# A hand-ordered encoder layer: another order for the first four rows of the sequence and for the last partial sums

## The chip, the core and the metric

One NeuronCore of one Trainium2 chip runs the whole layer in one launch. The metric is the device time of one execution in microseconds (us). The engines are named as in the profile: PE is TensorE (matmul), PEld its weight loads, DVE is VectorE, ACT is ScalarE, POOL is GpSimd, SP is SyncE, whose queue issues most DMAs.

## The reference

```python
memn = rms_norm(mem, mem_norm_g); h = x                       # x: (1, 512, 1024), mem: (1, 256, 1024)
n = rms_norm(h, mix_norm_g); proj = n @ w_in                  # 1024 -> 4608 columns
xa, zu, zv = proj[..., :512], proj[..., 512:1536], proj[..., 1536:2560]
gate_a, gate_b = sigmoid(proj[..., 2560:3584]), sigmoid(proj[..., 3584:])
ya = s5_branch(xa, ...)        # two scans over the sequence, GLU
yb = sgu_branch(zu, zv, ...)   # gelu, layer norm, 128x128 position mixing by head
h = h + (gate_a * (ya @ w_proj_a) + gate_b * (yb @ w_proj_b)) @ w_out
h = h + memory_cross_attention(rms_norm(h, xattn_norm_g), memn, w_q, w_k, w_v, w_xo)
n = rms_norm(h, ffn_norm_g); h = h + (silu(n @ w_gate) * (n @ w_up)) @ w_down
return rms_norm(h, final_norm_g)
```

All arrays are float32.

## The kernel before

**Products.** The 512 positions are four row tiles of 128 (t = 0 to 3). Each float32 operand is split into a high part in fp32r (a cast on ACT, `whi`, `xn_hi`) and the remainder (a subtraction on DVE, `wlo`, `xn_lo`); `mm3` makes a product of three passes: high by high, high by low of the second operand, low by high. `split` issues the cast and the subtraction. Weights come from HBM by SP's queue into `raw` tiles of 512 KB, three of them in rotation; `plan` lists every weight block in the order of use, and `next_w` loads ahead of the use and splits two blocks ahead (`SPLITS`). There are three `whi` and three `wlo` buffers, so a cast waits until PE has used the block three before.

**Order.** A scheduler that models the engines' times sets the order of the instructions on each engine. `in_order` (`tc.keep_in_program_order`) pins an instruction to the program's order, and `tc.issue_after(x)` puts the instructions of a block behind x on x's engine.

**The start (L617 to L692).** `g_mix` is the gain of the first norm, spread to 128 partitions by two matmuls into `pg`. `first_rows` norms and turns rows 0 and 1, pinned: the sums of squares of a row (`row_sums`, two ACT instructions), the factor r (`rms_factor`: two small DVE instructions and a power on POOL), the scaling by r and gain (`scaled`, on DVE, by halves of 512 columns), four transposes on PE into `ptr` (`to_feat`), and the split of `ptr` into `xn` (cast on ACT, subtraction on DVE). Among these stand the splits of the first three weight blocks w0, w1, w2 of `w_in` (`parts`, `split_w`), w0 by halves. Rows 2 and 3 follow in a loop, not pinned. The first product is `tokm` on `w_in` (four row tiles by 512 columns, two k blocks of 128 in each weight block). For row 0, the passes over w0 and w1 have an order of their own; an entry is (k block, part of `xn`, part of w):

```python
first=(((0, 0, 0), (0, 0, 1), (1, 0, 0), (0, 1, 0), (1, 1, 0), (1, 0, 1)),
       ((0, 0, 0), (1, 0, 0), (0, 1, 0), (1, 1, 0), (0, 0, 1), (1, 0, 1)))
```

`behind=turned1` puts row 0's passes over the later blocks behind the last transpose of row 1.

**The end (L1926 to L1984).** The down projection of the FFN is made of seven products (`DOWN`), each over six chunks of `w_down`. Products 7 and 4 are the last ones. `row_by_row` takes two chunks for row tile t = 0 and then for t = 1. After product 7, `onto_h` takes its two PSUM tiles `dx` off `h`, and `first_half(t, 0)` for t = 2, 3 makes the sum of squares of one half row (ACT), the half row times the last gain (DVE, `rest<-h,g_o`) and a small factor. Then product 4 goes over its chunks; its first two are again `row_by_row`.

Of the kernel before, what the change touches and what calls it, by code (L numbers as in the profile page):

```python
# [12 lines left out]
ALU = mybir.AluOpType  # L13
# [4 lines left out]
P = 128  # L18
D = 1024
T = 512  # L20
NT = T // P
# [31 lines left out]
def hybrid_layer_kernel(  # L53
# [38 lines left out]

    pinned, turned, row_tr = [False], [], [None]
    in_order = tc.keep_in_program_order
# [10 lines left out]
    def halves(src, place=None):  # L105
        _, k, n = src.shape
        if place is None:
            hi = wp.tile([P, k, n], F32R, tag="hi", name="whi", bufs=3)
            lo = wp.tile([P, k, n], F32R, tag="lo", name="wlo", bufs=3)
        else:  # L110
            hi, lo = sums_place(place, k, n)
        split(hi, lo, src)
        return hi, lo


# [17 lines left out]
    def plan_block(w, kb, k, c0, n, more=None, place=None, parts=1):  # L133
        got = {}

        def load():
            got["raw"] = wp.tile([P, k, n], F32, tag="raw", name="wraw", bufs=3)
            for i in range(0, k, k // parts):
                nc.sync.dma_start(got["raw"][:, i:i + k // parts], block(w, kb + i, k // parts, c0, n))

        def make():
# [247 lines left out]
    def load_raw(j):  # L389
        begin(j, j)  # L390
# [49 lines left out]
    def tokm(w, c0, act, nk, evac, ntok=NT, last=2, kpt=2, hook=None, cut=None, t0=0, behind=None, fine=False, first=()):  # L440
# [22 lines left out]
        for t in toks:  # L463
# [5 lines left out]
            else:  # L469
                with nullcontext() if behind is None or t > t0 else tc.issue_after(behind):  # L470
                    tok_block(ps[t], t, held, act, kpt, full, nw == last, True)
# [148 lines left out]
    nc.scalar.dma_start(xt[:, 0, HALF[1]], x[0:P, HALF[1]])  # L620
    for t in range(1, NT):
        load_raw(t - 1)
        nc.sync.dma_start(xt[:, t, :], x[t * P:(t + 1) * P])
    xn_hi, xn_lo = token_slot("xn")
    xn = (xn_hi, xn_lo)

    def first_rows():
# [9 lines left out]
        def gain_copy(q):  # L637
            in_order(nc.scalar.copy(g_mix[:, HALF[q]], pg[q]))

# [14 lines left out]
        scaled(0, 0, r, pg[0])  # L654
        gain_copy(0)
        high, low = parts(0)
        high(0)
        low(0)
        turn(0, 0)
        idles(3)  # L660
        high(1)
        low(1)
        scaled(0, 1, r, pg[1])
        r = rms_factor(row_sums(xt[:, 1, :]))
        high, low = parts(1)
# [8 lines left out]
        split_w(2)  # L674
        ss = row_sums(xt[:, 2, :])
        turn(1, 1)
        pinned[0] = False
        return ss

    ss = first_rows()  # L680
    turned1 = row_tr[0]
    ss3 = row_sums(xt[:, 3, :])
    for t in range(2, NT):
        r = rms_factor(ss)
        with tc.issue_after(turned[1].ins):
            for i in range(2):
                nc.vector.scalar_tensor_tensor(xt[:, t, HALF[i]], xt[:, t, HALF[i]], r, g_mix[:, HALF[i]], ALU.mult, ALU.mult)
        to_feat(xt[:, t, :], xn_hi, xn_lo, slice(t * P, (t + 1) * P))
        ss = ss3
    last_row = [x.ins for x in turned]  # L690
# [1234 lines left out]

    def onto_h(ps, t0, half, op):  # L1926
        for t in range(2):
            hs = h[:, t0 + t, HALF[half]]
            added = nc.vector.tensor_tensor(hs, hs, ps[t], op)
            first = added.ins if t == 0 else first  # L1930
        return first

# [26 lines left out]
    row_by_row(7, CHUNKS - 2)  # L1959
    held_back[0] = onto_h(dx, 2, 0, ALU.subtract)  # L1960
    for t in range(2, 4):
        first_half(t, 0)

    held = []
    row_by_row(4, 0)
    held_back[0] = None
    for c in range(2, CHUNKS):
        ops_ = next_w(w_down, 4, c)
        if c < CHUNKS - 2:
            rows_product(dx, 4, c, ops_, (0, 1), slice(0, 512), False, c == CHUNKS - 3)  # L1970
        else:
            held.append((c, ops_))
# [46 lines left out]
```

## Time and profile before

| | |
|---|---|
| median of 3 runs | 864.3 us (863.7 to 865.82) |
| profiled execution | 864.56 us |
| its span | 862.8 us |
| PE busy | 853.0 us, 5898 matmuls |
| DVE, ACT, POOL busy | 646.8, 475.1, 105.6 us |
| granted TensorE clock | 0.998 |

The profile is of one execution. Times in it are from the start of its span; 864.56 - 862.8 = 1.8 us of the execution's time lie around the span. A row of the timeline has the start, the duration, the engine, the line, the operation with out<-in, and in brackets the engine's idle time before it with what ended that; "x3" is three instructions merged into one row, whose duration is then that of the three together. A matmul's end is modelled; matmuls of 512 columns that wait for nothing start 0.23 us apart, transposes 0.11 us apart.

### The profile page before, as it was taken

Reading aid. Unit: us, or ns where it says so; the run is one execution under the profiler, and the core shown is the slowest. Engines: PE = TensorE matmul, PEld = TensorE weight load, DVE = VectorE, ACT = ScalarE, POOL = GpSimd, SP = SyncE. Lnnn points to the kernel's source line nnn. Section 1 sums busy time; section 2 is a strip of 40 time slices with the busy share of each in tenths; the row PEclk is TensorE's granted clock in tenths of the full one; section 3 lists DMA queues with packets and bytes.
Section 4 is the critical chain, followed back from the end, with each engine's and each line's share of the span. In section 5 each row is a group of like instructions: output and inputs, shape, how many; then the busy total and the mean of one; then the engine's idle time right before and its main releaser. Section 6 shows DMA issues by size and latency. Waiting matters only on the chain.

```text
span 862.8 us, 14842 instructions
## 1 busy us (share of the span) xinstructions
PE 853.0 (99%) x5898; PEld 760.4 (88%) x5898; DVE 646.8 (75%) x889; ACT 475.1 (55%) x704; POOL 105.6 (12%) x157
## 2 busy tenths in 40 slices
PE   8999999999999999999999999999999999999996
PEld 6788888888889988899899888999999999988885
DVE  5799589958848768679658556877876778899875
ACT  6544874276436644467557444655545454656573
POOL 1001155100611000110010000010111111000000
PEclk9999999999999999999999999999999999999999
DMA  7549379645638687945788153557699789686641
GB/s 242 176 110 259 77 191 273 155 124 192 158 91 228 170 221 227 259 124 151 219 250 227 59 168 77 147 150 181 162 230 236 190 221 240 181 232 204 199 153 49
DMA packets 110135, 155.40 MB, mean 180 GB/s; under 512 B 8985, under 2 KB 77105, under 8 KB 110002
## 3 DMA queue, kind: packets, MB, share of 16 engines
q1 hardware_dynamic: 91762, 128.27, 47.0%
q0 software_dynamic: 18016, 25.66, 18.8%
q8 instruction: 46, 0.75, 0.4%
q10 hardware_dynamic: 288, 0.52, 0.2%
q14 instruction: 23, 0.19, 0.1%
HBM read 148.70 MB, written 37.20 MB: 215 GB/s over the span
## 4 chain that ended last, share of the span: by engine, by line
PE 97%; DVE 1%; ACT 1%; issue 0%; DMA 0%; POOL 0%; POOLq 0%
PE pf L400 27%; PE pt L400 18%; PE px L1292 13%; PE pq L1292 6%; PE dx L400 6%; PE dq L400 3%; PE pv L1292 3%; PE gx L1292 3%; PE qx L1292 3%; PE dv L400 2%; PE py L1081 1%; PE psc L400 1%; PE po L400 1%; PE qq L1292 1%; PE gq L1292 1%; PE ptr L573 1%
## 5 line engine op out<-in xcount | busy, mean ns | idle before, releaser
L85 ACT CAST whi<-wraw 128x1024 fp32r<-128x1024 f32 x132 | 135.7, 1029 | 141.7 <-PE pf L400 37.7
L86 DVE TENSOR_TENSOR wlo<-wraw,whi 128x1024 fp32r<-128x1024 f32 x132 | 157.5, 1193 | 70.9 <-ACT whi L85 69.6
L400 PE MATMUL pf<-xn,whi 128*128 128x512 f32 x320 | 100.2, 393 | 0.0
L1292 PE MATMUL px<-fn,whi 128*128 128x256 f32 x480 | 83.3, 276 | 0.0
L1292 PEld LDWEIGHTS px<-fn,whi 128*128 128x128 f32 x480 | 72.5, 188 | 0.2
L86 DVE TENSOR_TENSOR wlo<-b,whi 128x1024 fp32r<-128x1024 f32 x40 | 48.9, 1223 | 29.4 <-ACT whi L85 29.4
L400 PEld LDWEIGHTS pf<-xn,whi 128*128 128x128 f32 x320 | 59.5, 188 | 12.6 <-issue 0.7
L85 ACT CAST whi<-b 128x1024 fp32r<-128x1024 f32 x40 | 42.1, 1053 | 51.7 <-PE px L1292 26.3
L1292 PE MATMUL px<-fn,wlo 128*128 128x256 f32 x240 | 66.4, 277 | 0.0
L400 PE MATMUL pf<-xn,wlo 128*128 128x512 f32 x160 | 62.7, 392 | 0.0
L1292 PE MATMUL pq<-s,whi 128*128 128x256 f32 x320 | 55.0, 276 | 0.0
L400 PE MATMUL dx<-whi,s 128*128 128x512 f32 x170 | 53.0, 390 | 0.0
L86 DVE TENSOR_TENSOR wlo<-t,whi 128x1024 fp32r<-128x1024 f32 x30 | 36.7, 1225 | 19.3 <-ACT whi L85 19.3
L85 ACT CAST whi<-t 128x1024 fp32r<-128x1024 f32 x30 | 31.6, 1054 | 35.2 <-PE pv L1292 12.6
L1292 PEld LDWEIGHTS pq<-s,whi 128*128 128x128 f32 x320 | 48.1, 188 | 0.0
L1292 PEld LDWEIGHTS px<-fn,wlo 128*128 128x128 f32 x240 | 45.1, 188 | 0.0
L1292 PE MATMUL pq<-s,wlo 128*128 128x256 f32 x160 | 44.2, 276 | 0.0
L400 PE MATMUL pt<-whi,xn 128*128 128x512 f32 x120 | 39.6, 401 | 0.3 <-ACT xn L85 0.2
L400 PEld LDWEIGHTS dx<-whi,s 128*128 128x128 f32 x170 | 31.8, 188 | 6.8 <-DVE s L86 0.3
L313 POOL DMA_DIRECT2D dsum<-in_w_down_dram x12 | 13.3, 1109 | 190.4 <-DMA dsum<-in_w_down_dram 190.4
L400 PEld LDWEIGHTS pf<-xn,wlo 128*128 128x128 f32 x160 | 30.0, 188 | 6.2
L400 PE MATMUL dx<-wlo,s 128*128 128x512 f32 x85 | 33.1, 391 | 0.9 <-DVE wlo L86 0.9
(484 smaller groups left out, 2331.7 us busy)
## 6 DMA issues: line engine op xcount, KB each, us to landing
wraw<-in_w_in_dram SPq DMA_DIRECT2D x34, 512.0 KB, 4.5
dsum<-in_w_down_dram SPq DMA_DIRECT2D x20, 512.0 KB, 6.5
wraw<-dsum SPq DMA_DIRECT2D x20, 512.0 KB, 3.7
b<-in_w_gate_dram SPq DMA_DIRECT2D x15, 512.0 KB, 5.4
b<-in_w_up_dram SPq DMA_DIRECT2D x15, 512.0 KB, 4.9
wraw<-in_w_down_dram SPq DMA_DIRECT2D x15, 512.0 KB, 4.8
dsum<-in_w_down_dram POOLq DMA_DIRECT2D x10, 512.0 KB, 7.6
dsum<-dsum POOLq DMA_DIRECT2D x10, 512.0 KB, 6.4
```

Source lines behind the costliest of these rows:

```text
L85: hi = nc.scalar.copy(dst_hi, src)
L86: lo = nc.vector.tensor_tensor(dst_lo, src, dst_hi.bitcast(F32), ALU.subtract)
L313: plan[j + step][1].append((0, lambda d=dst, x=more: nc.gpsimd.dma_start(d, x, accum_op=ALU.add)))
L400: last_mm[0] = nc.tensor.matmul(ps, a[x], b[y], start=start and i == 0, stop=stop and i == 2, skip_group_check=free)
L573: tr = nc.tensor.transpose(ps[:, j, :], src[:, k * P:(k + 1) * P], ident)
L1081: in_order(nc.tensor.matmul(ps[64 * j:64 * j + 64, :], a, b, start=g % 4 == k == 0, stop=k == 2, tile_position=(0, 64 * j), skip_group_che ...
L1292: nc.tensor.matmul(ps[:, j, :], a[x], b[y], start=start and j == k == i == 0, stop=k == 3 and i == 2, skip_group_check=True)
```

## The change

- **Queue of SP:** row 1 of x is loaded between the two halves of w0 (`row_load`), where it came behind both.
- **First rows:** the first half of `g_mix` is copied by DVE, behind `low(0)`, where ACT copied it ahead of `high(0)`. The scaling of row 0's second half and the sums and the factor of row 1 stand ahead of `high(1)` and `low(1)`, the split of the second half of w0.
- **Rows 2 and 3:** row 2's factor is made ahead of `turn(1, 1)`; row 3's sums are put behind the cast of `turn(1, 1)` on ACT; each half row is turned by a call of its own. `turned1` is a list now: in `tokm`, the last passes of row tile 0 stand behind the last transpose of row 1, those of row tile 1 behind the first half of row 2, those of row tile 2 behind the first half of row 3.
- **The end:** `split_log` keeps the instructions of each weight split. The second subtraction of `onto_h` after product 7 is put behind the `wlo` of the newest block split by then, and `first_half` of rows 2 and 3 is moved behind `row_by_row(4, 0)` and behind the second subtraction of `onto_h` and the split of a weight block. The tokens of later chunks wait for that second subtraction, where it was the first.

```diff
@@ halves
-        split(hi, lo, src)
+        split_log.append([x.ins for x in split(hi, lo, src)])
@@ plan_block, load
             for i in range(0, k, k // parts):
                 nc.sync.dma_start(got["raw"][:, i:i + k // parts], block(w, kb + i, k // parts, c0, n))
+                if parts > 1 and i == 0:
+                    row_load[0]()
@@ tokm
-                with nullcontext() if behind is None or t > t0 else tc.issue_after(behind):
+                with nullcontext() if behind is None or t - t0 >= len(behind) else tc.issue_after(behind[t - t0]):
@@ loads of x
-    for t in range(1, NT):
+    load_row = lambda t: nc.sync.dma_start(xt[:, t, :], x[t * P:(t + 1) * P])
+    row_load[0] = lambda: load_row(1)
+    load_raw(0)
+    for t in range(2, NT):
         load_raw(t - 1)
-        nc.sync.dma_start(xt[:, t, :], x[t * P:(t + 1) * P])
+        load_row(t)
@@ first_rows
         def gain_copy(q):
-            in_order(nc.scalar.copy(g_mix[:, HALF[q]], pg[q]))
+            in_order(nc.vector.tensor_copy(g_mix[:, HALF[q]], pg[q]) if q == 0 else
+                     nc.scalar.copy(g_mix[:, HALF[q]], pg[q]))
...
         scaled(0, 0, r, pg[0])
-        gain_copy(0)
         high, low = parts(0)
         high(0)
         low(0)
+        gain_copy(0)
         turn(0, 0)
         idles(3)
+        scaled(0, 1, r, pg[1])
+        r = rms_factor(row_sums(xt[:, 1, :]))
         high(1)
         low(1)
-        scaled(0, 1, r, pg[1])
-        r = rms_factor(row_sums(xt[:, 1, :]))
         high, low = parts(1)
...
         ss = row_sums(xt[:, 2, :])
+        r = rms_factor(ss)
         turn(1, 1)
+        turned1 = [row_tr[0]]
         pinned[0] = False
-        return ss
-    ss = first_rows()
-    turned1 = row_tr[0]
-    ss3 = row_sums(xt[:, 3, :])
-    for t in range(2, NT):
-        r = rms_factor(ss)
-        with tc.issue_after(turned[1].ins):
-            for i in range(2):
-                nc.vector.scalar_tensor_tensor(xt[:, t, HALF[i]], xt[:, t, HALF[i]], r, g_mix[:, HALF[i]], ALU.mult, ALU.mult)
-        to_feat(xt[:, t, :], xn_hi, xn_lo, slice(t * P, (t + 1) * P))
-        ss = ss3
+        with tc.issue_after(turned[0].ins):
+            ss = row_sums(xt[:, 3, :])
+        for t in range(2, NT):
+            with tc.issue_after(turned[1].ins) if t > 2 else nullcontext():
+                for i in range(2):
+                    sc = nc.vector.scalar_tensor_tensor(
+                        xt[:, t, HALF[i]], xt[:, t, HALF[i]], r, g_mix[:, HALF[i]], ALU.mult, ALU.mult)
+            r = rms_factor(ss) if t == 2 else None
+            turn(t, 0)
+            turned1.append(row_tr[0])
+            turn(t, 1)
+        return turned1
+    turned1 = first_rows()
@@ onto_h
-    def onto_h(ps, t0, half, op):
+    def onto_h(ps, t0, half, op, behind=None):
         for t in range(2):
             hs = h[:, t0 + t, HALF[half]]
-            added = nc.vector.tensor_tensor(hs, hs, ps[t], op)
-            first = added.ins if t == 0 else first
-        return first
+            with nullcontext() if behind is None or t == 0 else tc.issue_after(behind):
+                added = nc.vector.tensor_tensor(hs, hs, ps[t], op)
+        return added.ins
@@ after product 7
-    held_back[0] = onto_h(dx, 2, 0, ALU.subtract)
-    for t in range(2, 4):
-        first_half(t, 0)
+    held_back[0] = onto_h(dx, 2, 0, ALU.subtract, split_log[-1][1])
     held = []
     row_by_row(4, 0)
+    behind_all = [held_back[0]] + split_log[used_w[0] - 1 - len(tiles)]
     held_back[0] = None
+    with ExitStack() as waits:
+        for x in behind_all:
+            waits.enter_context(tc.issue_after(x))
+        for t in range(2, 4):
+            first_half(t, 0)
```

The orders of instructions move as follows. Lines are those of each kernel, so L533 before is L537 in the changed kernel, L648 is L656, L400 is L404, L479 is L483.

ACT at the start, before, from the sums of row 0: `sq,ss<-xt` are sums of squares, `whi<-wraw 128x512` the casts of w0's halves, `whi<-wraw 128x1024` those of w1 and w2, `xn<-ptr` the casts of turned half rows.

```order
L533 ACTIVATE sq,ss<-xt 128x512 x2
L638 COPY g_mix<-pg 128x512
L648 CAST whi<-wraw 128x512
L85 CAST xn<-ptr 128x4x128
L648 CAST whi<-wraw 128x512
L533 ACTIVATE sq,ss<-xt 128x512 x2
L648 CAST whi<-wraw 128x1024
L638 COPY g_mix<-pg 128x512
```

The same place in the changed kernel:

```order
L537 ACTIVATE sq,ss<-xt 128x512 x2
L656 CAST whi<-wraw 128x512
L85 CAST xn<-ptr 128x4x128
L537 ACTIVATE sq,ss<-xt 128x512 x2
L656 CAST whi<-wraw 128x512
L656 CAST whi<-wraw 128x1024
L646 COPY g_mix<-pg 128x512
```

The first copy of the gain is gone from ACT, and the two sums of row 1 have changed places with the cast of w0's second half.

PE from the second half of row 1 on, before: `ptr` are transposes, `pt0_262`, `pt1_263` and `pt2_264` the sums of row tiles 0, 1 and 2; `whi_194` and `wlo_195` are w2, `whi_146` is w0.

```order
L573 MATMUL ptr_203<-ident_87,xt_115 128x128 x4
L400 MATMUL pt0_262<-whi_194,xn_128 128x512
L400 MATMUL pt0_262<-wlo_195,xn_128 128x512
L400 MATMUL pt0_262<-whi_194,xn_128 128x512 x2
L400 MATMUL pt0_262<-wlo_195,xn_128 128x512
L400 MATMUL pt0_262<-whi_194,xn_128 128x512
L400 MATMUL pt1_263<-whi_194,xn_128 128x512
L400 MATMUL pt1_263<-wlo_195,xn_128 128x512
L400 MATMUL pt1_263<-whi_194,xn_128 128x512 x2
L400 MATMUL pt1_263<-wlo_195,xn_128 128x512
L400 MATMUL pt1_263<-whi_194,xn_128 128x512
L573 MATMUL ptr_222<-ident_87,xt_115 128x128 x4
```

In the changed kernel, where w0 is `whi_145`:

```order
L577 MATMUL ptr_208<-ident_87,xt_115 128x128 x4
L404 MATMUL pt0_262<-whi_194,xn_128 128x512
L404 MATMUL pt0_262<-wlo_195,xn_128 128x512
L404 MATMUL pt0_262<-whi_194,xn_128 128x512 x2
L404 MATMUL pt0_262<-wlo_195,xn_128 128x512
L404 MATMUL pt0_262<-whi_194,xn_128 128x512
L577 MATMUL ptr_227<-ident_87,xt_115 128x128 x4
L404 MATMUL pt1_263<-whi_194,xn_128 128x512
L404 MATMUL pt1_263<-wlo_195,xn_128 128x512
L577 MATMUL ptr_234<-ident_87,xt_115 128x128 x4
L404 MATMUL pt1_263<-whi_194,xn_128 128x512 x2
L404 MATMUL pt1_263<-wlo_195,xn_128 128x512
```

The eight transposes of row 2 have come apart into four ahead of row tile 1's passes over w2 and four behind the second of them; those of row 3 are parted in the same way around row tile 2's passes over w2.

DVE near the end, before: `wlo_8681` and `wlo_8687` are the low parts of the first two chunks of product 4, `h<-h,dx` the two subtractions of `onto_h`, `s2` the low part of the tokens for chunks 2 and 3, `rest<-h,g_o` belongs to `first_half`.

```order
L86 TENSOR_TENSOR wlo_8681<-wraw_8596,whi_8680 128x1024
L1929 TENSOR_TENSOR h_3419<-h_3419,dx0_7869 128x512
L86 TENSOR_TENSOR s2_8720<-a_low_5453,s2_8720 128x1024
L1889 TENSOR_TENSOR rest_7506<-h_3419,g_o_8009 128x512
L1890 TENSOR_SCALAR msq_8011<-hss_3434 128x1
L1929 TENSOR_TENSOR h_3419<-h_3419,dx1_7870 128x512
L86 TENSOR_TENSOR wlo_8687<-wraw_8622,whi_8686 128x1024
```

In the changed kernel:

```order
L86 TENSOR_TENSOR wlo_8681<-wraw_8596,whi_8680 128x1024
L1942 TENSOR_TENSOR h_3419<-h_3419,dx0_7869 128x512
L86 TENSOR_TENSOR wlo_8687<-wraw_8622,whi_8686 128x1024
L1942 TENSOR_TENSOR h_3419<-h_3419,dx1_7870 128x512
L86 TENSOR_TENSOR s2_8712<-a_low_5453,s2_8712 128x1024
L1901 TENSOR_TENSOR rest_7506<-h_3419,g_o_8009 128x512
L1902 TENSOR_SCALAR msq_8011<-hss_3434 128x1
```

The low part of chunk 1 has moved ahead of four instructions. On ACT at the same place the cast `whi_8686` has moved ahead of the sum of squares of `first_half`.

Behind the first rows the scheduler's order differs on all engines up to about the middle of the gates' products; the work is the same there, in other places. From there to the end of product 7, and behind product 4's first chunks, the orders are equal but for buffer numbers.

More of the change, by code (lines that the diff above doesn't have):

```diff
@@ L90, in split @@
         return hi, lo
-    pinned, turned, row_tr = [False], [], [None]
+    pinned, turned, row_tr, row_load = [False], [], [None], [None]
     in_order = tc.keep_in_program_order
@@ L111, in halves @@
             hi, lo = sums_place(place, k, n)
-        split(hi, lo, src)
+        split_log.append([x.ins for x in split(hi, lo, src)])
         return hi, lo
+    split_log = []
     APART = (48, 112)
```

## The prediction

> **What bounds the kernel now.** I read the page first, then the stretches, then who waits, and only then the timeline at the two places that the change touches. The page's busy line and five stretches (the columns are length, then busy time of PE, PEld, DVE, ACT and POOL, granted clock, DMA share, GB/s):
>
> ```profile
> PE 853.0 (99%) x5898; PEld 760.4 (88%) x5898; DVE 646.8 (75%) x889; ACT 475.1 (55%) x704; POOL 105.6 (12%) x157
> ...
> 8.59:14.00 5.41, 4.62 (x20) 3.03 (x21) 4.48 (x9) 4.06 (x9) 0.56 (x1) 1.00 1.04 333
> ...
> 40.00:60.00 20.00, 20.00 (x94) 16.56 (x93) 19.82 (x38) 10.00 (x21) 1.34 (x1) 1.00 0.56 151
> 60.00:100.00 40.00, 40.00 (x368) 33.55 (x367) 35.72 (x53) 24.85 (x38) 2.32 (x2) 1.00 0.71 184
> 100.00:840.00 740.00, 740.00 (x5193) 669.05 (x5192) 553.71 (x707) 407.68 (x583) 97.41 (x139) 1.00 0.68 184
> 840.00:843.00 3.00, 2.13 (x10) 1.47 (x9) 3.00 (x6) 2.85 (x6) 0.00 (x0) 1.00 0.00 0
> ```
>
> PE has no idle time between 40 and 840 us, at full clock. So the change can win only where PE stands still: in the first rows and at 840 to 843 us. All that PE waits for, from the view of waits (total, times, longest), says the same:
>
> ```profile
> PE dx L400 <- DVE wlo L86: 0.9, 1, 0.9
> PE pt L479 <- ACT whi L648: 0.7, 1, 0.7
> ```
>
> **The change, part by part. 1: row 0 and the first weights.** The timeline of before; each row is one step of the chain:
>
> ```profile
> 6.95 0.59 ACT L638 COPY g_mix<-pg 128x512 f32<-128x512 f32 x1 [1.86 <-DVE xt L634]
> 7.17 0.60 PE L573 MATMUL ptr<-ident,xt 128*128 128x128 f32 x4
> 7.95 0.59 ACT L85 CAST xn<-ptr 128x512 fp32r<-128x512 f32 x1
> 8.59 0.50 PE L479 MATMUL pt<-whi,xn 128*128 128x512 f32 x1
> 8.95 0.64 ACT L533 ACTIVATE sq<-xt 128x512 f32<-128x512 f32 x1
> 10.03 0.50 PE L479 MATMUL pt<-wlo,xn 128*128 128x512 f32 x1
> 10.19 1.03 ACT L648 CAST whi<-wraw 128x1024 fp32r<-128x1024 f32 x1
> 11.27 1.19 PE L479 MATMUL pt<-whi,xn 128*128 128x512 f32 x4 [0.74 <-ACT whi L648]
> 12.37 1.09 PE L573 MATMUL ptr<-ident,xt 128*128 128x128 f32 x8
> 13.50 0.72 PE L479 MATMUL pt<-wlo,xn 128*128 128x512 f32 x2
> 14.54 0.62 PE L400 MATMUL pt<-whi,xn 128*128 128x512 f32 x2
> ```
>
> The gain copy leaves ACT, so the cast of `xn` waits for the transposes alone. Row 2's, below, has its cast 0.64 us after the first transpose (20.04 to 20.68); by that it starts at 7.17 + 0.64 = 7.81, and the first product at 8.59 - 0.14 = 8.45. On DVE the copy is new. No DVE copy of this shape from PSUM is in the trace; its bounds are ACT's 0.59 above and the 0.68 of a DVE subtraction from PSUM (shown at 840.48 below). It starts behind `low(0)`, which no longer waits for the gain copy, and either way ends by about 8.4, ahead of the 8.45 at which `xn_lo` can start; its price is nothing, or up to 0.2 if the first weight half lands late.
>
> Now the two sums of row 1 come ahead of the second cast of w0. Steps on ACT as now (cast to next 0.48, two sums 1.24 from 8.95 to 10.19): sums from 8.29, second half cast from 9.53 to 10.16. PE's third pass needs it and moves from 9.1 to 10.21: a new hole of 1.1 us. The next three passes follow at 0.34, 0.23 and 0.23, the last at 11.01. The cast of w1 runs from 10.05 to 11.08; PE asks for it at 11.24. So the hole of 0.74 closes and the sum of both is near zero: four passes to 11.93, transposes at 12.16 in place of 12.37. That is -0.21, because the scaling of row 1 (needed here) is done at about 11.55, a POOL power earlier than now. The next wait also goes: `wlo` of w1 now ends at 12.68, so passes go on at 13.15 in place of 13.50; and row 1's pass with `xn_lo` stands at 14.18 in place of 14.54: **-0.36**.
>
> All this needs row 1 of x by 8.29. The view of DMAs around 2.5 us has the time from issue to landing:
>
> ```profile
> xt<-in_x_dram SPq DMA_DIRECT2D x1, 512.0 KB, 6.0
> wraw<-in_w_in_dram SPq DMA_DIRECT2D x1, 256.0 KB, 4.6
> ```
>
> The first was issued at 2.49 and landed at 8.48, the second (w0's second half, ahead of it) at 2.02 and 6.66: 1.82 us for the 512 KB behind it. With 256 KB less ahead I estimate a landing at 8.48 - 0.7 to 0.9 = 7.6 to 7.8, and no wait. If it stayed at 8.48, the term would shrink by 0.2. [...] The landings above agree with the queue's order, so I keep the first.
>
> **2: rows 2 and 3.**
>
> ```profile
> 16.68 0.15 DVE L542 TENSOR_TENSOR ms<-ss 128x1 f32<-128x1 f32 x1
> 16.83 0.60 PE L573 MATMUL ptr<-ident,xt 128*128 128x128 f32 x4
> 17.17 0.55 POOL L544 TENSOR_TENSOR r<-ms,mhalf 128x1 f32<-128x1 f32 x1 [5.64 <-DVE ms L543]
> 17.18 0.48 PE L400 MATMUL pt<-whi,xn 128*128 128x512 f32 x1
> 18.08 0.69 DVE L86 TENSOR_TENSOR xn<-ptr,xn 128x512 fp32r<-128x512 f32 x1 [0.17 <-ACT xn L85]
> 18.69 1.41 DVE L687 SCALAR_TENSOR_TENSOR xt<-xt,r,g_mix 128x512 f32<-128x512 f32 x2
> 20.04 1.03 PE L573 MATMUL ptr<-ident,xt 128*128 128x128 f32 x8
> 20.68 1.08 ACT L85 CAST xn<-ptr 128x512 fp32r<-128x512 f32 x2 [2.62 <-PE ptr L573]
> 21.32 0.50 PE L400 MATMUL pt<-whi,xn 128*128 128x512 f32 x1 [0.24 <-ACT xn L85]
> 22.04 0.30 PEld L400 LDWEIGHTS pt<-whi,xn 128*128 128x128 f32 x2 [0.43 <-DVE xn L86]
> ```
>
> Now row 2 is turned late: PE goes from the transposes straight to passes that need them, and waits for cast and subtraction (its weight load, PEld, shows the second wait; 20.04 to 22.04 is 2.00 us for eight transposes and two passes; 8 x 0.11 + 2 x 0.23 = 1.34 would do). After: r of row 2 is done 0.24 earlier, at 17.48, as DVE's chain is; its scaling stands ahead of row 1's last `xn_lo` and runs 17.53 to 18.94. PE has six passes of row tile 0 from 16.81 to 18.27, waits at most 0.1 for the first half row, turns it (0.35, as 16.83 to 17.18), does two passes, turns the second half, and does the last four passes of row tile 1 (behind `xn_lo` of row 1, now late, at 19.5; PE comes there at 19.5). Meanwhile row 2 is cast and subtracted, by 20.5 for the first half. Row tile 2 starts at 20.55 and its third pass comes at 21.0 in place of 22.04: **-1.0** with the -0.36 in it. Row 3 is the same with no wait in it now; a group of four transposes and the switch back costs 0.35 + 0.09, so parting eight costs 0.2 more or less. I take **-0.95** for the start, from -0.2 (landing late, the new hole longer than the old) to -1.3.
>
> **3: the end.**
>
> ```profile
> 838.82 0.62 PE L400 MATMUL dx<-whi,s 128*128 128x512 f32 x2
> 838.79 0.63 ACT L533 ACTIVATE sq<-h 128x512 f32<-128x512 f32 x1 [0.94 <-DVE h L1929]
> 839.42 1.98 ACT L85 CAST whi<-wraw 128x1024 fp32r<-128x1024 f32 x2
> 840.48 0.68 DVE L1929 TENSOR_TENSOR h<-h,dx 128x512 f32<-128x512 f32 x1
> 841.07 1.22 DVE L86 TENSOR_TENSOR wlo<-wraw,whi 128x1024 fp32r<-128x1024 f32 x1
> 842.35 0.50 PE L400 MATMUL dx<-wlo,s 128*128 128x512 f32 x1 [0.87 <-DVE wlo L86]
> ```
>
> The cast of chunk 1 (839.42) waits for PE to leave its buffer: the first of the two passes at 838.82 is the last user and ends at 838.82 + 0.39 = 839.21. Without the sum of squares ahead it starts at 839.27 and ends at 840.3; the low part, no longer behind `rest` and the second subtraction, runs 840.35 to 841.57, and PE goes on at 841.62 in place of 842.35: **-0.73**. PE would ask at 841.3, so 0.3 stays. What is late next: the token low part moves from 838.7 to about 842.1 to 843.3; its first use is behind the last pass of 24 over chunks 0 and 1, after 845.8. The low part of chunk 2 ends at 845.2, used at 846.0. Both covers hold with 0.8 us or more. Bounds -0.5 to -0.9 (0.87 is the whole wait).
>
> **4: the middle**, up to about 285 us, is shuffled by the scheduler. PE has nothing to win there but small switches. The one queue with a new wait is POOL: its accumulating DMA of `qsum`, which waits for SP's transfer, now stands ahead of the layer norm's powers:
>
> ```profile
> 124.21 1.21 POOL L313 DMA_DIRECT2D qsum<-in_w_q_dram  x1 [2.50 <-DMA qsum<-in_w_q_dram]
> ...
> 125.70 2.18 ACT L1194 ACTIVATE zt<-zt,r 128x1024 f32<-128x1024 f32 x2
> ...
> L1256 PE MATMUL psv<-wsx,zt x17: 270/275/275, 148.1 to 149.9; 128*128 128x128 f32 x17
> ```
>
> The first power can then not start before about 125.4, ACT's scaling slips by up to 1 to 2 us, and the weight casts queued behind it; PE uses `zt` only at 148.1, and splits run two blocks ahead. I price it at 0, up to 1.
>
> **The sum:** -0.95 - 0.73 + 0 = -1.7 us against this execution's 864.56: 862.9. It lies 0.26 above the median, so the forecast against 864.3 is **862.6 us**. Bounds together (-0.2 - 0.5 + 1, and -1.3 - 0.9) give +0.3 to -2.2.
>
> **The rivals.**
> *The middle gives too.* If the new order also closes switches and short waits between 28 and 290 us, another 1.3 us: 861.3. For: each change from 512-column passes to small products costs about 0.1 to 0.2. Against: PE reads 100% there, and the changed order has three such groups more, not fewer.
> *DVE late, slower.* In 40 to 60 us DVE is busy 19.82 of 20.00, and in 60 to 100 35.72 of 40. The new order puts some four weight subtractions (1.22 each) ahead of products of the S5 branch, whose results PE's queue takes at fixed places with the dense passes behind. If PE gets there first, each costs up to 1.22, 4.9 in all: 862.6 + 4.9 = 867.5. It decides where that slip is more than the lead that the products have now; PE's zero idle there says that today's lead is enough, not how large it is.
> *The start does not do what it should.* The new hole at 9.1 to 10.2 grows by a late landing, and the gain of row 2 is lost on the late `xn_lo` of row 1: only the end remains, 864.3 - 0.73 = 863.6.
> *The clock falls.* PE now stands for 1.1 us after only two passes, right after the warm-up matmuls; if the grant halved, about six passes would take 0.23 longer each, 1.4: 864.0. The grant is 1.00 in 8.59 to 14.00 with a hole of the same length in it. [...]
>
> **How the numbers follow.** About 0.3%, 2.6 us, is what a measurement of this kernel can tell from no change: below 861.7 is faster, above 866.9 slower. Forecast 0.56 (its own range 861.2 to 863.7), of which 0.12 lies below 861.7, since the medians of three runs here scatter by some 0.7; the middle gives too 0.22, all faster; the start fails 0.08 and the clock 0.04, both the same; DVE late 0.10, slower. Faster 0.34, same 0.56, slower 0.10. The range of 860.9 to 864.8 leaves out DVE late and the tails.
>
> **What would show it.** Right: the first product at 8.45, the third pass near 10.2, no wait for ACT at w1, row tile 2's third pass near 21.0, PE's wait for `wlo` near 842 down to 0.3. Wrong: PE waits for S5 products between 40 and 290 us, or row 1's sums starting after 8.5.

## The result, and the profile after

Over 12 executions each the kernel after takes 869.14 us (866.02 to 871.62) and the kernel before 865.36 us (863.7 to 866.75), medians; the ratio is 1.0041, 95% interval 1.0028 to 1.0055. The change makes the kernel 0.4% **slower**; 0.2% faster was forecast. The profiled execution took 867.14 us with a span of 865.4, 2.58 us more than that of before.

One thing has to be known to read the times below: the executions of every kernel here, before's too, fall in two groups 2 to 3 us apart, by how fast PE's passes are at the start (the four that broadcast g take 2.14 us in before's profile and 3.78 in that of experiment 1; the last section shows the rows), so kernels are compared within a group. Groups are parted at the widest gap in a kernel's sorted times (in 8 at the second widest, since its profiled execution, of 865.83 us, has a late start: its first product comes at 11.11). After's early group is at 867.17 (5 executions) against 864.28 (6), its late one at 870.45 (7) against 866.48 (6). The fastest execution of after, 866.02, stands 1.1 us below the next one; it was not profiled, and what it was spared is not known.

From the page of after, the busy line:

```profile
PE 853.9 (99%) x5898; PEld 761.9 (88%) x5898; DVE 648.2 (75%) x890; ACT 475.1 (55%) x703; POOL 103.5 (12%) x157
```

The stretches of after, with the columns of the prediction:

```profile
8.35:14.00 5.65, 4.64 (x22) 3.16 (x22) 4.72 (x9) 4.42 (x10) 0.55 (x1) 1.00 1.07 356
...
60.00:100.00 40.00, 40.00 (x370) 34.04 (x369) 35.83 (x53) 24.92 (x37) 2.32 (x2) 1.00 0.65 172
100.00:840.00 740.00, 737.39 (x5169) 666.55 (x5169) 551.27 (x703) 405.02 (x577) 95.31 (x139) 1.00 0.66 184
843.00:846.00 3.00, 2.87 (x13) 2.03 (x13) 2.34 (x3) 3.00 (x7) 0.00 (x0) 1.00 0.00 0
```

The end is nearly closed (2.87 of 3 us busy, where it was 2.13), but PE now stands still for 2.6 us between 100 and 840, where it never did. All that PE waits for after, from the view of waits:

```profile
PE gx L1304 <- ACT u L1313: 2.4, 1, 2.4
PE idle L612 <- DVE level L880: 1.1, 1, 1.1
PE pt L483 <- ACT whi L656: 1.0, 1, 1.0
PE pf L404 <- DVE yb_lo L86: 0.2, 1, 0.2
```

The first line is new: the products of the gate weights (`gw`, `gx`). So is the last. The second line is at the very start and stands in before's view too, with the same 1.1 us. The stretches around it, after, show what it drags behind it in the column of the granted clock:

```profile
284.00:287.00 3.00, 0.55 (x6) 0.36 (x4) 1.52 (x2) 2.60 (x4) 0.00 (x0) 1.00 0.74 119
...
288.00:290.00 2.00, 2.00 (x13) 2.00 (x12) 2.00 (x3) 0.94 (x2) 0.00 (x0) 0.57 0.00 0
290.00:292.00 2.00, 2.00 (x13) 2.00 (x12) 0.17 (x1) 0.75 (x1) 0.00 (x0) 0.58 0.60 199
292.00:294.00 2.00, 2.00 (x19) 2.00 (x18) 1.67 (x2) 0.80 (x2) 0.00 (x0) 1.00 0.18 64
```

Between 288 and 292 PE is busy, yet starts 13 matmuls in 2 us and not 19, at a clock of 0.57. To add the losses up, I compare the two traces at points where PE has carried out the same set of matmuls (after minus before):

| PE has done the same up to (time before) | after minus before |
|---|---|
| 31.8, first rows | -1.24 |
| 216.8, just ahead of the wait for `yb_lo` | -1.54 |
| 217.7, behind it | -1.09 |
| 271.2, second gate product | -0.53 |
| 285.0, behind the hole | +1.95 |
| 288.3, clock up again | +3.45 |
| 842.3, PE's wait for `wlo` at the end | +2.59 |

So the start won 1.5 us and the end 0.75, both as forecast or better; the middle lost 1.0 in small pieces, 2.5 in one hole and 1.5 by a low clock.

**The hole, row by row.** ACT casts the next gate weights as soon as an accumulating DMA into `gw` has landed; behind that cast, and a second one, stands its copy of `gx` into `u`, which frees the PSUM tile that PE's next pass writes. From the timeline of before, ACT's two rows, PE's pass and POOL's two DMA issues:

```profile
282.44 2.00 ACT L85 CAST whi<-gw 128x1024 fp32r<-128x1024 f32 x2 [4.01 <-PE gx L1292]
284.35 0.58 ACT L1301 COPY u<-gx 128x512 f32<-128x512 f32 x1
284.98 0.51 PE L1292 MATMUL gx<-xn,whi 128*128 128x256 f32 x2
271.74 1.20 POOL L313 DMA_DIRECT2D dsum<-in_w_down_dram  x1 [32.27 <-DMA dsum<-in_w_down_dram]
273.14 1.35 POOL L257 DMA_DIRECT2D gw<-in_w_in_dram  x1 [0.20 <-issue]
```

and from before's view of DMAs the last of them, its time from issue to landing at the end of the row:

```profile
gw<-in_w_in_dram POOLq DMA_DIRECT2D x1, 512.0 KB, 9.2
```

The DMA landed at 273.14 + 9.2 = 282.34, the cast started at 282.44, the copy ended at 284.93, PE went on at 284.98. PE shows no idle time there, and in this execution there was no slack either: every link was just in time. The same rows of after's timeline:

```profile
284.40 1.99 ACT L85 CAST whi<-gw 128x1024 fp32r<-128x1024 f32 x2 [6.51 <-PE gx L1304]
286.30 0.58 ACT L1313 COPY u<-gx 128x512 f32<-128x512 f32 x1
286.93 0.50 PE L1304 MATMUL gx<-xn,whi 128*128 128x256 f32 x2 [2.45 <-ACT u L1313]
272.63 1.20 POOL L317 DMA_DIRECT2D dsum<-in_w_down_dram  x1 [31.20 <-DMA dsum<-in_w_down_dram]
273.99 1.35 POOL L261 DMA_DIRECT2D gw<-in_w_in_dram  x1 [0.16 <-issue]
```

and of its view of DMAs:

```profile
gw<-in_w_in_dram POOLq DMA_DIRECT2D x1, 512.0 KB, 10.3
```

The landing is 1.96 us later (273.99 + 10.3 = 284.3) and PE arrives 0.53 earlier: 2.5 us. The releaser given for the cast (PE, 6.51) had long been done; the DMA is the one that came last. The first of POOL's two rows belongs to another job, an advance sum of `w_down` (`dsum`) that is used hundreds of us later. It waits for its own load, and that load went late, as SP's queue shows in the timeline of before:

```profile
258.29 4.75 SPq L1440 DMA_DIRECT2D gat<-gad  x4
263.08 0.60 SPq L312 DMA_DIRECT2D dsum<-in_w_down_dram  x1
264.02 5.34 SPq L240 DMA_DIRECT2D wraw<-in_w_in_dram  x2
```

and of after:

```profile
259.41 1.39 SPq L1452 DMA_DIRECT2D gat<-gad  x3
264.54 0.37 SPq L244 DMA_DIRECT2D wraw<-in_w_in_dram  x1
265.00 1.49 SPq L1452 DMA_DIRECT2D gat<-gad  x1
266.53 0.60 SPq L316 DMA_DIRECT2D dsum<-in_w_down_dram  x1
```

The scheduler now puts a load of gate weights ahead of the fourth `gat` load, and the load of `dsum` goes 3.45 us later.

### The profile page after: what moved, and what is told of

Same layout as the page of the kernel before. It is cut to its first block, busy times and chain, and to the rows that moved or that the text cites. A ratio compares the mean times of both kernels' runs of the same rounds, so it can differ in the third digit from the quotient of the medians.

```text
span 865.4 us, 14842 instructions
## 1 busy us (share of the span) xinstructions
PE 853.9 (99%) x5898; PEld 761.9 (88%) x5898; DVE 648.2 (75%) x890; ACT 475.1 (55%) x703; POOL 103.5 (12%) x157
## 4 chain that ended last, share of the span: by engine, by line
PE 96%; ACT 1%; DVE 1%; issue 1%; POOLq 0%; POOL 0%; ACTq 0%
PE pf L404 25%; PE pt L404 18%; PE px L1304 13%; PE dx L404 6%; PE pq L1304 6%; PE dq L404 3%; PE pv L1304 3%; PE gx L1304 3%; PE qx L1304 3%; PE dv L404 2%; PE ptr L577 1%; PE psc L404 1%; PE gq L1304 1%; PE po L404 1%; PE py L1093 1%; PE qq L1304 1%
## 5 line engine op out<-in xcount | busy, mean ns | idle before, releaser
L404 PE MATMUL pf<-xn,whi 128*128 128x512 f32 x320 | 100.4, 393 | 0.0
L404 PEld LDWEIGHTS pf<-xn,whi 128*128 128x128 f32 x320 | 59.6, 188 | 12.6 <-issue 0.5
L404 PE MATMUL pf<-xn,wlo 128*128 128x512 f32 x160 | 62.9, 393 | 0.0
L404 PE MATMUL dx<-whi,s 128*128 128x512 f32 x170 | 53.0, 390 | 0.0
L404 PE MATMUL pt<-whi,xn 128*128 128x512 f32 x120 | 40.1, 402 | 0.0
L404 PEld LDWEIGHTS dx<-whi,s 128*128 128x128 f32 x170 | 31.8, 188 | 6.7 <-DVE s L86 0.3
L404 PEld LDWEIGHTS pf<-xn,wlo 128*128 128x128 f32 x160 | 30.1, 188 | 6.1 <-issue 0.2
L404 PE MATMUL dx<-wlo,s 128*128 128x512 f32 x85 | 33.0, 390 | 0.1
```

The source lines that it names most:

```text
L404: last_mm[0] = nc.tensor.matmul(ps, a[x], b[y], start=start and i == 0, stop=stop and i == 2, skip_group_check=free)
```

## The experiments

Times in us; "early" and "late" are the medians of the two groups, with the number of executions. Where a kernel has one or two in a group, that number says little. Before was timed again beside each series (1 to 4, 5 to 8, 9 to 11).

| kernel | median | early | late | before: early, late | ratio of all (95%) |
|---|---|---|---|---|---|
| 1 sum behind, after | 865.67 | 863.19 (2) | 865.81 (10) | 864.40, 866.64 | 0.9992 (0.998 to 1.0003) |
| 2 sum behind, before | 866.47 | 864.35 (3) | 866.49 (9) | same | 0.9999 (0.999 to 1.0009) |
| 3 one load later, before | 866.65 | 864.40 (4) | 867.38 (8) | same | 1.0004 (0.9991 to 1.0016) |
| 4 the end alone | 863.45 | 863.39 (6) | 865.97 (1) | same | 0.9978 (0.9965 to 0.9992) |
| 5 rows 2, 3 as before | 865.62 | 863.57 (1) | 865.68 (11) | 864.43, 866.49 | 1.0 (0.9989 to 1.0011) |
| 6 loads as before | 865.49 | 863.43 (2) | 865.54 (10) | same | 0.9997 (0.9986 to 1.0007) |
| 7 gains apart | 864.44 | 863.49 (9) | 866.91 (3) | same | 0.9991 (0.9977 to 1.0005) |
| 8 gains apart, end alone | 863.78 | 863.69 (8) | 865.83 (3) | same | 0.9987 (0.9975 to 1.0) |
| 9 rows 2, 3 alone | 870.3 | 868.32 (1) | 870.39 (4) | 864.25, 866.28 | 1.005 (1.0036 to 1.0063) |
| 10 after again | 868.74 | 867.16 (6) | 869.86 (6) | same | 1.0033 (1.002 to 1.0046) |
| 11 gains apart, rows as before | 865.6 | 863.17 (6) | 867.18 (6) | same | 1.0 (0.9985 to 1.0015) |

**1 and 2: the add for `w_down` behind the add into `gw`, in the kernel after and in the kernel before.** Nothing else moves on any engine.

```diff
-                    nc.gpsimd.dma_start(t, b(1, 0), accum_op=ALU.add)
+                    gate_adds.append(nc.gpsimd.dma_start(t, b(1, 0), accum_op=ALU.add).ins)
...
+        def add(d, x, j):
+            with tc.issue_after(gate_adds[0]) if j >= 50 else nullcontext():
+                nc.gpsimd.dma_start(d, x, accum_op=ALU.add)
...
+            plan[j + step][1].append((0, lambda d=dst, x=more, j=j: add(d, x, j)))
```

> The kernel after, with one thing exchanged: on POOL's queue the add that completes the first sum for w_down stands behind the first of the two adds into gw (the gate weights) and no longer ahead of it. Theory (POOL's queue): in the kernel after, the add into gw could have gone at 269.4, when DVE had done its part, and went at 273.99 because the add for w_down ahead of it waited for a load that SP issued 3.45 us later than before. With the exchange it is issued near 269.5 and lands by 279, PE has no hole at 284 (2.5 us) and no low clock behind it (1.45 us): 4 us less than the kernel after, about 864 where before has 865.4. Rival (crowded DMA): the add into gw lands late because the transfers beside it are many, whichever stands first; then a hole of 1 to 2 us stays and the time is 866 to 868. Rival (elsewhere): the median of the kernel after lies 2 us above its profiled execution for reasons in another place; then less than 1.5 us of the 3.8 come back.

> The kernel before, with the same exchange on POOL's queue. Theory: before, the add into gw landed at 282.34 and its cast started at 282.44, just in time, so nothing waited; an earlier landing gives 0 in the profiled execution, and at most 1 us in the median if the executions near 866.5 are those in which it landed later. Rival (the place always costs): a gain of over 1 us.

POOL's queue in the timeline of the first (its profiled execution is a late one, so times stand about 2.9 us later than those of after):

```profile
275.91 1.37 POOL L261 DMA_DIRECT2D gw<-in_w_in_dram  x1 [31.58 <-issue]
276.71 1.79 POOL L317 DMA_DIRECT2D dsum<-in_w_down_dram  x1
```

Its view of DMAs:

```profile
gw<-in_w_in_dram POOLq DMA_DIRECT2D x1, 512.0 KB, 5.8
```

The hole is gone, and with it the low clock (1.00 in every stretch from 284 to 296): PE waits nowhere in the middle but 0.2 us for `yb_lo`. In the late group the kernel after falls from 870.45 to 865.81, its early one from 867.17 to 863.19: 4.6 and 4.0 us, where 4 were expected. But not for the reason that I gave. The add could not have gone at 269.4, because DVE was not yet done with the old content of `gw`. In the eight profiles in which the add did not queue behind `dsum` (1, 2, 4 to 8 and 11) it goes 1.15 us after the end of one low part on DVE (in 4 that ends at 270.62 + 1.22 = 271.84, the add goes at 273.00). In the kernel after this low part ends at 271.88, so the add could have gone at 273.0, and POOL's queue held it back by 1.0 us only. What shrank is the transfer: 5.8 us from issue to landing, where it takes 10.3 with the 512 KB of `dsum` 1.36 us ahead of it on the same queue. The rival that put it on crowded transfers was nearer, though which of the two stands first does matter. In the kernel before the exchange brings nothing (864.35 and 866.49 against 864.40 and 866.64), as expected where nothing waited.

These two runs also show what the rest of the change is worth. Both profiles are late ones without a hole. At equal sets of matmuls the first is 0.9 us ahead of the second at 201 us, 0.2 behind it at 285 and 0.7 ahead of it behind the end. In this pair the small losses of the middle take all that the start wins, and what stays is the end.

**3: one load of gate weights ahead of the load of `dsum`, in the kernel before.** No other order is changed.

```diff
-                    nc.sync.dma_start(got[nm], src)
+                    gate_loads.append(nc.sync.dma_start(got[nm], src).ins)
...
+        def load(d, x, j):
+            with tc.issue_after(gate_loads[-2]) if j >= 50 else nullcontext():
+                tc.keep_in_program_order(nc.sync.dma_start(d, x))
...
+            plan[j][1].append((0, lambda d=dst, x=src, j=j: load(d, x, j)))
```

> The kernel before, with one thing moved: on SP's queue the first load for the sums of w_down stands one load of gate weights later, as it does in the kernel after. Nothing of the start or the end is changed. Theory: that load goes about 1.4 us later, the add for w_down and the add into gw behind it on POOL about 1 to 1.4 us later, the gate cast with them; before had no slack there, so PE gets a hole of 1 to 2 us near 285 and a lower clock for some us behind it: 1.5 to 3.5 us slower than before. Rival (crowded DMA): the landing moves by less than 0.5 us and the time stays within 0.5 us of before.

The profile has a hole again, of 1.2 us from pass to pass. From its view of waits, then from its view of DMAs:

```profile
PE gx L1296 <- ACT u L1305: 1.0, 1, 1.0
```

```profile
gw<-in_w_in_dram POOLq DMA_DIRECT2D x1, 512.0 KB, 10.0
```

The add into `gw` was issued at 275.80 and before at 273.14; this execution's first product came 2.46 later (a late one), so 0.2 us of that is new. It landed 10.0 us after its issue and not 9.2, and these 0.8 us make most of the hole. It was smaller than I expected, the clock stayed up behind it (1.00 in every stretch from 284 to 296), and the cost is 0 to 0.7 us by group. Four executions of twelve, the profiled one among them (867.86 to 868.34), lie above the highest of before (867.43), the others where before's lie. So the direction fits the theory, the size does not, and with one profile it is not shown that the step on SP's queue opened this hole: the time of that transfer also differs between executions of one order (under 10).

**4: the end of the change alone**, on the kernel before.

```diff
-    held_back[0] = onto_h(dx, 2, 0, ALU.subtract)
-    for t in range(2, 4):
-        first_half(t, 0)
+    held_back[0] = onto_h(dx, 2, 0, ALU.subtract, split_log[-1][1])
...
+        for t in range(2, 4):
+            first_half(t, 0)
```

> The kernel before, with the end of the change alone: the second subtraction into h behind wlo of the weight split, and the first halves of the last rows behind the passes of product 4. No order ahead of the last 25 us is changed. Theory: the wait at 841 shrinks by 0.73 us as the trace of the kernel after shows, and the whole is 0.7 us faster than before. Rival: the half rows that now go later are late at the very end, and 0.3 us or less is left.

PE's wait for `wlo` of 0.9 us is in its view of waits no more; 0.3 us are left between the passes there. It is 1.0 us faster in the early group and 0.7 in the one late execution, and at equal sets of matmuls PE gains 0.74 at the end against before's profile; the theory holds. The ratio of all exaggerates it, because 6 of its 7 executions were early ones and only 11 of 31 of before.

**5: rows 2 and 3 as before, all else of the change kept.** The block of the loop over rows 2 and 3 is put back. **9: rows 2 and 3 changed alone**, the reverse.

> The kernel after, with rows 2 and 3 scaled and turned as before (their factor, their order and the passes that they stand ahead of); the loads, the copy of g, row 1's sums and the end stay as changed. From the waits of row 2 on, the orders of the middle are those of before, the fourth gat load stands ahead of the gate weights on SP again. Theory (the turned rows reshuffle the middle): no hole at 284, no low clock behind it, but of the start's gain only the first 0.3 to 0.6 us is left; with 0.75 us of the end this is 1.0 to 1.4 us faster than before, and 3 to 5 us faster than the kernel after. Rival (a shift of the start alone moves the add into gw late, the transfers being where they were in time): a hole of over 1 us near 284 stays and the time is within 0.5 us of before or above it.

> The kernel before with the change of rows 2 and 3 alone (their factor early, their halves turned apart and ahead of passes, the passes behind them); loads, copy of g, row 1's sums and the end as before. The orders of the middle are then those of the kernel after. Theory (the turned rows reshuffle the middle): the add into gw goes late on POOL again, PE has a hole of 2 to 3 us near 285 and a low clock behind it, 4 to 5 us in all with 1 us lost at 215 and 250; the start gains 0.6 to 1.0 us, the end nothing: 3 to 4.5 us slower than before, and about 1 us slower than the kernel after beside it. Rival (it takes the earlier first rows too): the hole is under 1 us, the time within 1 us of before.

POOL's queue in the timeline of 5:

```profile
272.84 1.20 POOL L317 DMA_DIRECT2D dsum<-in_w_down_dram  x1 [31.61 <-DMA dsum<-in_w_down_dram]
275.22 1.35 POOL L261 DMA_DIRECT2D gw<-in_w_in_dram  x1 [1.18 <-issue]
```

The same of 9, and then its longest wait, from the view of waits:

```profile
274.90 1.20 POOL L313 DMA_DIRECT2D dsum<-in_w_down_dram  x1 [30.56 <-DMA dsum<-in_w_down_dram]
276.26 1.35 POOL L257 DMA_DIRECT2D gw<-in_w_in_dram  x1 [0.16 <-DVE part L1371]
```

```profile
PE gx L1296 <- ACT u L1305: 2.6, 1, 2.6
```

These two settle where the loss comes from. With the rows as before there is no hole (`gw` lands 6.3 us after its issue), and 0.8 to 0.9 us are won; with the rows alone there is the whole hole (2.6 us, with a clock of 0.50 in 290 to 292 and 0.78 in 292 to 294), and 4.1 us are lost in either group (868.32 to 864.25, 870.39 to 866.28). The second is what the theory expected, the first a little less. Rows 2 and 3 stand in the first 30 us, and what they cost is 250 us later: what ties the two is the scheduler's order and, for about 0.5 us, that PE comes there earlier.

**6: loads as before.** Row 1 of x behind both halves of w0, on the kernel of experiment 1.

> The kernel after with the add into gw ahead on POOL (as in the first experiment), and with row 1 of x loaded behind both halves of w0 as before, not between them. Theory (the second half of w0 is what the new hole of 1.2 us at the start waits for): row 1 lands as before (about 0.8 us later than after), the second half of w0 earlier, so the pass that waits from 8.7 to 10.1 starts about where ACT's sums of row 1 let it, which are now later: within 0.3 us of the first experiment. Rival (the new order of loads is what the start gains by): 0.5 us or more slower than the first experiment.

865.54 against 865.81 in the late group: the new order of the first loads brings nothing that can be seen. ACT's sums of row 1 started at 10.64 and 10.65 in the two profiles, both late ones, long after row 1 had landed. In an early execution it may count for some tenths (863.43 against 863.19, two executions each); that is not shown.

**7, 8 and 11: the second half of g broadcast later,** on the kernels of experiments 1, 4 and 5. This is not a test of the change but of the two groups.

```diff
-        for i in range(2):
+        def gains(i):
             in_order(nc.tensor.matmul(pg[i], ones[0:1, :], g_row[:, HALF[i]], start=True, stop=True))
-        idles(1)
+
+        gains(0)
+        idles(5)
...
         turn(0, 0)
-        idles(3)
+        gains(1)
```

> The kernel of the first experiment, with the product that broadcasts the second half of g behind the transposes of row 0 in place of three idle products, and five idle products in its place ahead of them: as many instructions as before, two of the four passes of one row exchanged with idle products. Executions of every kernel fall in two groups about 2 us apart, by whether the clock of TensorE is up at 4.8 us or only at 11 to 12 us; in the late ones the four passes of one row take 3.8 us. Theory (passes of one row don't count as work for the clock): the clock comes up earlier in more of the executions, and the median falls by 1 to 2 us against the first experiment, the fastest executions staying within 0.3 us. Rival (the phase alone decides, whatever is run there): the same two groups in like shares, the same median within 0.5 us.

> The kernel before with the end of the change alone, as in the fourth experiment, and the same exchange of idle products and the second half of g as in the run beside it. Theory (passes of one row don't count): the late group becomes rarer, median 863.0 to 864.0. Rival (phase alone): the fastest near 863.3 as in the fourth experiment, the others near 865.5, in like shares as before has them.

> The kernel of the fifth experiment (rows 2 and 3 as before, all else of the change kept) with the second half of g broadcast behind row 0's transposes and the idle products ahead, as in the seventh. Theory: 0.9 us faster than before in the executions with an early clock, as the fifth was (about 863.5), and more of them, so a median of 863.5 to 864.5. Rival (phase alone): a median near 865.6 as in the fifth.

Early executions were 9 of 12, 8 of 11 and 6 of 12, against 2 of 12, 6 of 7 and 1 of 12 without it. That speaks for the theory in the first and the third pair, but before itself had 6 of 12, 11 of 31, 17 of 34 and 9 of 23 unchanged, and the late ones became later (867.18 in 11 against 865.68 in 5). It stays open, and the median of 11 is no better than that of 5. That the clock makes the two groups is an estimate too (the last section says from what), and "phase" in the rivals means no more than that the groups come whatever PE runs there.

**10: after again.**

> The kernel after, unchanged, so that its profile and its times stand beside those of the experiments of this call. Theory: again a hole of 1.5 to 3 us at 284 to 287 (later by what the clock came up later at the start), the add into gw issued 4 us or more after DVE's part; 3 to 4 us slower than before. Rival (the hole was a single execution's): no hole over 0.5 us, and the time is within 1 us of before.

A hole of 2.4 us again, `gw` landing 10.4 us after its issue, a clock of 0.53 and 0.61 in 290 to 294; 2.9 us slower than before in the early group, 3.6 in the late. Thirteen profiles, before's and after's among them, give one picture: with 2.4 us or more from the issue of `dsum` to that of `gw` (experiments 4, 5, 8, 11), or `gw` first (1, 2, 6, 7), `gw` lands in 5.8 to 6.3 us; with 1.4 us (before, after, 3, 9, 10) in 9.2 to 10.6. Why 1 us more between the two makes such a difference is not shown.

It also puts before's profile in its place. Experiments 4, 5, 8 and 11 have before's order on POOL, and there the add of `dsum` went 2.4 to 3.1 us ahead. From the timeline of 4:

```profile
269.94 1.20 POOL L315 DMA_DIRECT2D dsum<-in_w_down_dram  x1 [31.68 <-DMA dsum<-in_w_down_dram]
273.00 1.35 POOL L259 DMA_DIRECT2D gw<-in_w_in_dram  x1 [1.86 <-issue]
```

`gw` landed at 278.9 there, 3.4 us earlier than in before's profile, where the add of `dsum` came 8.7 us after SP issued its load (263.08 to 271.74) and not 7.0. So before's order has some 3 us to spare in four profiles of five and none in the fifth; with the changed rows and `dsum` ahead, the two adds stood 1.4 us apart and PE waited in all three profiles (after, 9, 10).

## Why the prediction was wrong, step by step

**The step that failed is the fourth, the middle "priced at 0, up to 1".** It cost 5.0 us (from -1.54 to +3.45). I took PE's 100% between 40 and 840 us to mean that the middle could lose only by new switches, and looked at one queue, POOL's at 124 us. Full busy time says that nothing waited in that execution, not by how much it was early. The rows that show it were in before's trace: a landing at 282.34, a cast at 282.44, a copy that ended 0.05 us ahead of PE's pass. The change's order on SP and POOL at that place, three rows that stand otherwise, was there to be read too. How narrow it was in before's trace is in part luck of that execution, since in experiment 4 the same transfer landed 3.4 us earlier; that the change uses up what is spare there is what experiments 1, 9 and 10 show. The one wait that was priced cost nothing: ACT's scaling of `zt` starts at 125.10, where it was 125.70.

Its parts, measured: the hole 2.5 us, of which 0.53 is the gain of the start itself, since PE came earlier to a transfer that did not; the clock behind it 1.5; small losses 1.0, of which 0.45 are lost around PE's wait for `yb_lo` at 215. In both kernels a product of the S5 branch (`etmp`) runs on DVE shortly ahead of it. Before:

```profile
214.68 1.22 DVE L912 TENSOR_TENSOR etmp<-raw_c,pe 128x1024 f32<-128x1024 f32 x1
215.92 0.69 DVE L86 TENSOR_TENSOR yb_lo<-zu,yb_hi 128x512 fp32r<-128x512 f32 x1
```

After:

```profile
213.90 1.22 DVE L924 TENSOR_TENSOR etmp<-raw_c,pe 128x1024 f32<-128x1024 f32 x1
215.04 0.69 DVE L86 TENSOR_TENSOR yb_lo<-zu,yb_hi 128x512 fp32r<-128x512 f32 x1
215.78 0.50 PE L404 MATMUL pf<-yb_lo,whi 128*128 128x512 f32 x1 [0.17 <-DVE yb_lo L86]
```

DVE's `yb_lo` ends 0.88 us earlier than before (215.73 and 216.61), PE comes there 1.54 us earlier. The other losses, another 0.55 us up to 271, I did not test.

**The steps that held.** Part 1: the first product was forecast at 8.45 and came at 8.35, the third pass at 10.21 and came at 10.09, the transposes at 12.16 and came at 12.07, and no wait for the cast of w1 is left. Row 1 of x landed at 7.65 (issued at 2.03, 5.6 us), forecast 7.6 to 7.8:

```profile
8.35 0.50 PE L483 MATMUL pt<-whi,xn 128*128 128x512 f32 x1
...
10.09 0.97 PE L483 MATMUL pt<-whi,xn 128*128 128x512 f32 x3 [1.01 <-ACT whi L656]
...
12.07 0.49 PE L577 MATMUL ptr<-ident,xt 128*128 128x128 f32 x3
...
21.05 0.62 PE L404 MATMUL pt<-whi,xn 128*128 128x512 f32 x2
```

Part 2: the third pass of row tile 2 came at 21.05, forecast 21.0. The start as a whole won 1.24 us by 31.8 and 1.5 by 65, where -0.95 was taken and -1.3 was the bound: the passes behind row 3 gained too. Part 3: 0.75 us for -0.73, with 0.3 left as forecast. Two notes on the reading: the prediction shows two of the four lines of its view of PE's waits (the others are 1.1 us at the very start and 0.2 for `xn` near 21), and the range of 860.9 to 864.8 is wider than the bounds of its sum, which give 862.1 to 864.6.

**The rivals.** "DVE late" named 867.5, close to the profiled 867.14, but by another mechanism: what waits is ACT's cast for a DMA, and DVE's part of the loss is 0.45. "The clock falls" was priced at the start, where in after's profile it did not fall behind a wait of 1.0 us (1.00 in every stretch up to 16 us); it fell in the middle. What before's trace shows for setting it aside is less than I made of it: in 8.59 to 14.00, at 1.00, the longest wait is 0.74 us and not the 1.1 forecast, and what a longer one does was not shown. Behind a wait of 2.4 to 2.6 us the granted clock was down in three profiles of three: 0.57 and 0.58 in 288 to 292 of after, 0.50 and 0.78 in 290 to 294 of 9, 0.53 and 0.61 in 290 to 294 of 10. Behind the 1.0 us of 3 it was 1.00. Nor is a wait the whole of it: in the profile of 4 the granted clock is 0.50 between 8 and 11 us with no wait of PE ahead of it in its view of waits but the 1.1 us at the very start. One of its stretches:

```profile
9.00:10.00 1.00, 1.00 (x4) 0.74 (x4) 1.00 (x3) 1.00 (x3) 0.00 (x0) 0.50 0.99 397
```

PE had run four passes of one row shortly before (1.98 us from 4.64 on); whether that is the reason stays open. "The start fails" and "the middle gives" did not come about.

**A version that beats both** is the end alone (4): 0.7 to 1.0 us better than before within the groups, with no order changed ahead of the last 25 us. The whole change with the sum's add behind (1) does 1.2 us in two early executions and 0.8 in ten late ones; by the times, the two can't be told apart.

## What to carry to other kernels

An engine that is 100% busy shows that nothing it needs is late, not that anything is early: before an order far ahead is touched, look for the transfers that land just as their user asks, in more than one profile, and list what stands ahead of them in each queue. Where a scheduler sets the order, a change of the first microseconds can move a DMA hundreds of microseconds later; compare the orders of the DMA queues, not only those of the engines that compute. A transfer that is needed soon belongs ahead of one that is needed late on the same queue (experiment 1: 4 us), and an edit that leaves all other orders alone (the end, here) keeps its gain.

## What the hardware showed that I had not expected

**Two starts.** The four passes that broadcast g begin at 4.77 in the timelines of before and of experiment 1. Before:

```profile
4.77 2.14 PE L631 MATMUL pg<-g_row,ones 1*128 1x512 f32 x4
```

Experiment 1:

```profile
4.77 3.78 PE L642 MATMUL pg<-g_row,ones 1*128 1x512 f32 x4
```

They take 2.14 us in the one and 3.78 in the other, where single passes of 512 columns still take 0.77 and 0.63 us at 11.06 and 11.63; before's first two take 0.50 and 0.40, at 8.59 and 8.93. That the clock is what differs is my estimate: in the profile of 4 the first two take 0.80 and 0.63 us, at 8.51 and 9.10, in stretches with a granted clock of 0.50. The record of the clock does not show it, since the stretches from 0 to 16 us have 1.00 in before as in experiment 1. The first product comes at 11.06; in the profile of after, whose start it has, it comes at 8.35. In experiment 2, whose middle is as before's, 2.0 us are left at 844. The start differs between executions of one kernel, with 2 to 3 us as the distance of the two groups; why there are two is not shown. For differences of 1 us a median over both groups is of little use, since it goes by how many executions of each group it caught.

**Two accumulating transfers on POOL's queue.** The 512 KB of this add into `gw` land 5.8 to 6.3 us after the issue when they go first or 2.4 us or more behind those of `dsum`, and 9.2 to 10.6 us when `dsum` was issued 1.4 us ahead. That the place counts and not the tile is shown by experiment 1, where `dsum`, then 0.8 us behind `gw`, takes 10.2.
